# Plain-float32 scores beside their projections, step sizes transposed in two parts, and key ends packed over two heads

## The chip, the cores and the metric

The kernel runs as one launch on one core of a Trainium2 chip. The core has five engines that the profile names: PE (TensorE, the matrix engine; PEld is its loading of weights), DVE (VectorE), ACT (ScalarE), POOL (GpSimd) and SP (SyncE, which issues the DMAs here). The metric is the device time of one execution, in microseconds (us).

## The reference, cut to what matters

A block of two branches (compressed, selected and windowed attention, and a gated branch) is followed by two more layers: one with a state-space branch (called SSD below) and a 31-tap convolution, one with neighbourhood attention. Three places in it matter here.

```python
# first block: scores of every head against 15 compressed keys
s_cmp = einsum(q, k_cmp) * 64 ** -0.5          # 256 tokens, 16 heads in 2 key groups
# middle layer: step sizes of 2 directions x 32 heads, and their running sums
dt = softplus(h @ w_dt + dt_bias)              # 64 rows x 272 tokens
cs = cumsum(dt * -exp(A_log))                  # one direction runs backwards
# last layer, 32 heads of 64: a token sees the 16 columns around it, all 4 rows, and 16 meta tokens
s = q @ k.T * 64 ** -0.5 + bias                # -inf outside the neighbourhood
o = softmax(s) @ v
```

The batch is 1, the sequence 256 tokens on a grid of 4 rows and 64 columns, the meta tokens 16, the model width 2048; everything is float32.

## The kernel before, in words

Activations lie transposed, features on the 128 partitions and tokens along the free axis: 256 columns in the first block, 272 (16 meta tokens and 256) behind it. A **projection** is one block of 128 output features: `proj` (L135) runs 16 chunks of the contraction, and for each of them `mm3` (L118 to L122) issues three matmuls into one accumulator `acc`: high part by high part, low by high, high by low, all in float32r. The parts come from `load_piece` (L90): a DMA brings 8 chunks of raw weights, ACT copies them to `wh` (L98) and DVE subtracts to `wl` (L99). So a projection is 48 matmuls and two weight pieces, and one weight piece feeds 24 matmuls. Whatever else PE does stands between these matmuls in its list.

A tile scheduler turns the program text into one fixed instruction list for each engine. `K.run(gen, n)` lowers the priority of a small task by n instructions (`LATER`, 1000 and 1500), so that the scheduler lets it float in between later work. `tap` (L831) puts one of 480 VectorE taps of the 31-tap convolution behind each `wl`. PSUM has three `acc` tiles, two of tag "t", one of tag "o" and one of tag "s".

- **Scores of the compressed branch** (`block1`): keys stand in `kcbd`, block-diagonal over the two key groups, as a high and a low tile. Eight projections `pj(0.125)` make the queries; `K.split` parts each of them into `qh` and `ql`. Behind the last, 16 blocks (2 token tiles by 8 query blocks) of 3 matmuls each write 128 x 32 scores into `scps`: 48 matmuls.
- **Step sizes** (`layer_e`, generator `steps`): DVE works out `dt`, then `la`, two scans give `cs`; then both are transposed in one step into tiles `dtp`: each has two transposes (L803) and four small matmuls (L806) for the first 32 tokens. `dtT` and `dt0` are read by `decay` (L898) in the SSD stage, which runs from about 1200 to 1560 us.
- **`norm_out`** (L719): 16 multiplies on DVE (L721) and four stores, another task that floats.
- **Last layer** (`layer_o`): 16 head pairs, four projections each (q, k, v, z). Query tile 0 sees keys 0 to 175 and tile 1 keys 96 to 271 (`KR`): 176 keys a head, two heads block-diagonal, 352 columns of scores in `sp`, a softmax along the keys in `sb`. For the product with v the keys are cut in 128 and 48 (`VR`): four transposes of `vf` into `vt_ps`, eight of the probabilities into `pt_ps` (L1188, L1189), and eight matmuls (L1195), each of 64 output partitions (one head), into `o_ps`.

Of the kernel before, what the change touches and what calls it, by code (L numbers as in the profile page):

```python
# [19 lines left out]
P = 128  # L20
# [233 lines left out]
def block1(K, a):  # L254
# [4 lines left out]
    with ExitStack() as ctx:  # L259
# [123 lines left out]
        kcbd = [wk.tile([P, 2, 2, 16], F32R, tag="kcbd%d" % i, bufs=1, name="kcbd%d" % i) for i in range(2)]  # L383
        for i in range(2):
            nc.vector.memset(kcbd[i].bitcast(F32), 0.0)
# [19 lines left out]
        for g in range(2):  # L405
            gs = slice(64 * g, 64 * g + 64)
            K.split(kcbd[0][gs, :, g, 0:15], kcbd[1][gs, :, g, 0:15],
                    cps[gs, :32].rearrange("q (p n) -> q p n", p=2)[:, :, 0:15])
            for p in range(2):
                nc.vector.tensor_copy(hidbd[gs, p, :, g, 0:15], hs[gs, 1, p, None, 0:15].to_broadcast([64, 4, 15]))  # L410
# [25 lines left out]
        scps = K.ps.tile([P, 2, S], F32, tag="t", bufs=2, name="scps")  # L436
        for t in range(2):
            ts = slice(128 * t, 128 * t + 128)
            for j in range(8):
                p = j // 4  # L440
                K.mm3(scps[:, t, 32 * j : 32 * j + 32].rearrange("q (g n) -> q g n", g=2), qh[:, j, ts], ql[:, j, ts],
                      kcbd[0][:, p], kcbd[1][:, p], True, True)
# [235 lines left out]
def layer_e(K, a):  # L678
# [3 lines left out]
    with ExitStack() as ctx:  # L682
# [88 lines left out]

        def steps():
            nc.vector.tensor_scalar(s_, e, 2.0, None, op0=ALU.add)
            yield 1.0
            nc.vector.reciprocal(s_, s_)
            yield 1.0
            nc.vector.tensor_tensor(s_, s_, e, op=ALU.mult)
            yield 1.0
            nc.vector.tensor_tensor(s2, s_, s_, op=ALU.mult)
            yield 1.0  # L780
            nc.vector.tensor_scalar(pl, s2, 1.0 / 15, None, op0=ALU.mult)
            yield 1.0
# [12 lines left out]
            nc.vector.tensor_tensor_scan(cs[0:32, :], on[0:32, :], la[0:32, :], 0.0, op0=ALU.mult, op1=ALU.add)
            yield 1.0
            nc.vector.tensor_tensor_scan(cs[32:64, ::-1], on[32:64, :], la[32:64, ::-1], 0.0, op0=ALU.mult, op1=ALU.add)
            yield 1.0
            nc.sync.dma_start(csd, cs)
            for k, src in enumerate((dt, cs)):  # L800
                tp = K.ps.tile([P, 512], F32, tag="t", bufs=2, name="dtp")
                for i, (s0, s1) in enumerate(TT2[1:]):
                    nc.tensor.transpose(tp[:, 64 * i : 64 * i + 64], src[:, s0:s1], K.ident[:64, :64])  # L803
                for q in range(4):
                    r0 = 32 * (q // 2) + q % 2
                    nc.tensor.matmul(tp[32 * q : 32 * q + 32, 128:144], src[:, 0:32], K.ident[:64, r0 : r0 + 31 : 2],  # L806
                                     start=True, stop=True, skip_group_check=True)
                nc.scalar.activation(dtT[:, k].rearrange("p i r -> p (i r)"), tp[:, 0:128], AF.Copy)
                nc.scalar.activation(dt0[:, k], tp[:, 128:144], AF.Copy)
            yield 1.0  # L810
# [282 lines left out]
def layer_o(K, a, out):  # L1093
# [5 lines left out]
    KR = [(0, 176), (96, T2)]  # L1099
    VR = [(0, 128), (128, 176), (96, 224), (224, T2)]  # L1100
    with ExitStack() as ctx:
# [28 lines left out]

        for i in range(16):
            bias = wk.tile([P, 2, 2, 176], F32, tag="bias", name="bias")
# [16 lines left out]
            vf = k1("vf")  # L1149
            nc.vector.tensor_tensor(vf, vp, rb, op=ALU.mult)  # L1150
            vt_ps = K.ps.tile([P, 4, P], F32, tag="t", bufs=2, name="vt_ps")
            vt = wk.tile([P, 4, P], F32, tag="vt", name="vt")
            for j, (s0, s1) in enumerate(VR):
                nc.tensor.transpose(vt_ps[: s1 - s0, j, :], vf[:, s0:s1], K.ident)
            nc.scalar.activation(vt[:, 0::2, :], vt_ps[:, 0::2, :], AF.Copy)
            nc.scalar.activation(vt[:48, 1::2, :], vt_ps[:48, 1::2, :], AF.Copy)
# [9 lines left out]
            for t in range(2):  # L1166
                ts = slice(128 * t, 128 * t + 128)
                k0, k1_ = KR[t]
                K.mm3(sp[:, t, :352].rearrange("p (g k) -> p g k", g=2), qh[:, ts], ql[:, ts],
                      kb[:, 0, :, k0:k1_], kb[:, 1, :, k0:k1_], True, True)  # L1170
            sb = wk.tile([P, 2, 2, 176], F32, tag="sb", name="sb")
            nc.vector.tensor_tensor(sb.rearrange("p t g k -> p t (g k)"), sp[:, :, :352],
# [10 lines left out]
            for t in range(2):  # L1183
                ts = slice(128 * t, 128 * t + 128)
                pt_ps = K.ps.tile([P, 2, 2, P], F32, tag="t", bufs=2, name="pt_ps")
                for g in range(2):
                    nc.vector.tensor_scalar(sb[:, t, g], sb[:, t, g], rs[:, t, g : g + 1], None, op0=ALU.mult)
                    nc.tensor.transpose(pt_ps[:, 0, g, :], sb[:, t, g, 0:128], K.ident)  # L1188
                    nc.tensor.transpose(pt_ps[:48, 1, g, :], sb[:, t, g, 128:176], K.ident)  # L1189
                pt = wk.tile([P, 2, 2, P], F32, tag="pt", name="pt")  # L1190
                nc.scalar.activation(pt[:, 0], pt_ps[:, 0], AF.Copy)
                nc.scalar.activation(pt[:48, 1], pt_ps[:48, 1], AF.Copy)
                for kt, n in ((0, 128), (1, 48)):
                    for g in range(2):
                        nc.tensor.matmul(o_ps[64 * g : 64 * g + 64, ts], vt[:n, 2 * t + kt, 64 * g : 64 * g + 64], pt[:n, kt, g, :],  # L1195
                                         start=kt == 0, stop=kt == 1, skip_group_check=True)
# [52 lines left out]
def prep(inp):  # L1249
# [79 lines left out]
    o["rpb"] = np.ascontiguousarray(bias.reshape(16, 2, P, 2, 176).transpose(0, 2, 3, 1, 4))  # L1329
# [50 lines left out]
```

## Time and profile before

| | |
|---|---|
| median of 3 runs | 2284.5 us (2283.99 to 2286.28) |
| profiled execution | 2284.89 us, of which the span is 2283.1 us |
| granted TensorE clock, mean | 0.990 of full speed |
| busy share | PE 98%, PEld 95%, DVE 71%, ACT 51%, POOL 5% |
| DMA | 174 GB/s on average over the span |
| chain that ended last | 94% of it on PE, 3% DVE, 2% ACT |

A busy share is the time in which an engine had at least one instruction under way; PE's instructions overlap (a matmul of 256 columns is shown with 0.28 us, and the next starts 0.12 us behind it), so what a matmul costs is read from start to start. In the page's list of groups the time of one matmul is therefore longer than what it adds to the span. A plain-float32 matmul appears as two records where a float32r one appears as one.

### The profile page before, as it was taken

How to read it: one execution, taken by the hardware profiler on the slowest of the kernel's cores; microseconds unless marked ns; L12 is line 12 of the kernel's file. 1: busy time of each engine (PE TensorE's matmuls, PEld its weight loads, DVE VectorE, ACT ScalarE, POOL GpSimd, SP SyncE). 2: the span in 40 equal slices, each digit the busy share in tenths (PEclk: the TensorE clock that was granted, in tenths of full speed). 3: DMA queues.
4: the chain of work that ended last, by engine and by line, in shares of the span. 5: the costliest groups of instructions: out<-in, count | busy, mean ns of one | idle time of the engine just before them, and what ended most of it. 6: DMA issues, size and time to landing. Idle time of an engine off the chain costs nothing.

```text
span 2283.1 us, 44200 instructions
## 1 busy us (share of the span) xinstructions
PE 2229.3 (98%) x17798; PEld 2159.0 (95%) x17798; DVE 1628.3 (71%) x2840; ACT 1164.8 (51%) x2087; POOL 124.7 (5%) x119
## 2 busy tenths in 40 slices
PE   8999999999999999999998998899999999999997
PEld 6998799999999998999998998899999999999997
DVE  6567777555555669999999888798766555565554
ACT  4446644444444444445547887745444545454453
POOL 1000000000000130000000010002011000000011
PEclk9999999999999999999999999999999999999999
DMA  7642455555556555554554555354655555545453
GB/s 260 226 153 94 133 191 183 187 186 186 187 195 209 183 165 195 198 175 166 177 175 145 171 172 189 120 177 153 202 176 188 170 168 169 169 162 167 159 174 121
DMA packets 126413, 398.20 MB, mean 174 GB/s; under 512 B 16832, under 2 KB 33664, under 8 KB 125696
## 3 DMA queue, kind: packets, MB, share of 16 engines
q1 hardware_dynamic: 126064, 395.36, 52.5%
q8 instruction: 140, 2.29, 0.4%
q14 instruction: 65, 0.53, 0.1%
q10 hardware_dynamic: 144, 0.01, 0.0%
HBM read 390.92 MB, written 4.40 MB: 173 GB/s over the span
## 4 chain that ended last, share of the span: by engine, by line
PE 94%; DVE 3%; ACT 2%; issue 1%; DMA 0%; POOL 0%; SPq 0%; DVEq 0%; ACTq 0%; POOLq 0%
PE acc L120 29%; PE acc L122 28%; PE acc L121 28%; PE acc L156 2%; PE o_ps L1195 1%; PE yps L956 1%; DVE wl L99 1%; DVE vb L842 0%; PE pt_ps L503 0%; PE sp L120 0%; ACT wh L98 0%; PE sp L122 0%; PE sp L121 0%; PE o_ps L509 0%; DVE xin L291 0%
## 5 line engine op out<-in xcount | busy, mean ns | idle before, releaser
L98 ACT ACTIVATE wh<-raw 128x1024 fp32r<-128x1024 f32 x674 | 713.2, 1059 | 967.9 <-PE acc L121 575.6
L99 DVE TENSOR_TENSOR wl<-raw,wh 128x1024 fp32r<-128x1024 f32 x674 | 828.9, 1231 | 383.7 <-ACT wh L98 376.2
L120 PE MATMUL acc<-uh,wh 128*128 128x272 f32 (+1 forms) x1488 | 437.8, 294 | 15.7 <-DVE za L992 8.7
L122 PE MATMUL acc<-uh,wl 128*128 128x272 f32 (+1 forms) x1488 | 437.5, 294 | 0.0
L121 PE MATMUL acc<-ul,wh 128*128 128x272 f32 (+1 forms) x1488 | 435.1, 292 | 0.0
L121 PE MATMUL acc<-xl,wh 128*128 128x256 f32 (+1 forms) x1136 | 322.3, 284 | 0.0
L120 PE MATMUL acc<-xh,wh 128*128 128x256 f32 (+1 forms) x1136 | 322.2, 284 | 0.0
L122 PE MATMUL acc<-xh,wl 128*128 128x256 f32 (+1 forms) x1136 | 321.2, 283 | 0.0
L120 PEld LDWEIGHTS acc<-uh,wh 128*128 128x128 f32 (+1 forms) x1488 | 282.7, 190 | 21.5 <-DVE za L992 9.5
L121 PE MATMUL acc<-oul,wh 128*128 128x256 f32 (+1 forms) x1024 | 294.4, 287 | 0.0
L122 PE MATMUL acc<-ouh,wl 128*128 128x256 f32 (+1 forms) x1024 | 294.0, 287 | 0.0
L120 PE MATMUL acc<-ouh,wh 128*128 128x256 f32 (+1 forms) x1024 | 292.8, 286 | 0.0
L122 PEld LDWEIGHTS acc<-uh,wl 128*128 128x128 f32 (+1 forms) x1488 | 282.1, 190 | 3.5 <-issue 2.3
L121 PEld LDWEIGHTS acc<-ul,wh 128*128 128x128 f32 (+1 forms) x1488 | 282.4, 190 | 1.7 <-issue 0.8
L120 PEld LDWEIGHTS acc<-xh,wh 128*128 128x128 f32 (+1 forms) x1136 | 213.8, 188 | 1.2 <-DVE pj L316 0.4
L122 PEld LDWEIGHTS acc<-xh,wl 128*128 128x128 f32 (+1 forms) x1136 | 214.4, 189 | 0.2
L121 PEld LDWEIGHTS acc<-xl,wh 128*128 128x128 f32 (+1 forms) x1136 | 213.6, 188 | 0.7 <-issue 0.4
L122 PEld LDWEIGHTS acc<-ouh,wl 128*128 128x128 f32 x1024 | 192.6, 188 | 2.6 <-issue 2.6
L121 PEld LDWEIGHTS acc<-oul,wh 128*128 128x128 f32 x1024 | 192.7, 188 | 0.2
L120 PEld LDWEIGHTS acc<-ouh,wh 128*128 128x128 f32 x1024 | 192.8, 188 | 0.0
L842 DVE SCALAR_TENSOR_TENSOR vb<-early,par,vb 128x257 f32<-128x257 f32 (+9 forms) x330 | 148.4, 493 | 0.9 <-ACT vb L826 0.7
L204 POOL TENSOR_TENSOR sq<-sq 128x272 f32<-128x272 f32 (+1 forms) x44 | 48.5, 1103 | 747.5 <-ACT sq L201 746.7
(413 smaller groups left out, 4290.7 us busy)
## 6 DMA issues: line engine op xcount, KB each, us to landing
raw<-in_e_w_in SPq DMA_DIRECT2D x184, 512.0 KB, 4.0
raw<-in_w_in_fm SPq DMA_DIRECT2D x140, 512.0 KB, 3.9
raw<-in_o_w_in SPq DMA_DIRECT2D x128, 512.0 KB, 4.1
raw<-in_e_w_out SPq DMA_DIRECT2D x64, 512.0 KB, 4.5
raw<-in_w_up SPq DMA_DIRECT2D x32, 512.0 KB, 3.9
raw<-in_w_out SPq DMA_DIRECT2D x32, 512.0 KB, 4.4
raw<-in_w_pg SPq DMA_DIRECT2D x32, 512.0 KB, 3.8
raw<-in_o_w_out SPq DMA_DIRECT2D x32, 512.0 KB, 4.5
```

The lines of the kernel that those rows point to most:

```text
L98: nc.scalar.activation(wh, raw, AF.Copy)
L99: ins = nc.vector.tensor_tensor(wl, raw, wh.bitcast(F32), op=ALU.subtract)
L120: mm(out, lh, rh, start=start, stop=False)
L121: mm(out, lh, rl, start=False, stop=False)
L122: mm(out, ll, rh, start=False, stop=stop)
L156: self.nc.tensor.matmul(a, raws[c // 8][:, c % 8, :], x(c), start=c == 0, stop=c == 15)
L204: self.nc.gpsimd.tensor_tensor(acc, acc, sq, op=ALU.add)
L842: ins = nc.vector.scalar_tensor_tensor(v[:, lo:hi], u[:, lo + o : hi + o], par(K, "e_dw_w", 31 * b + k), v[:, lo:hi], op0=ALU.mult, op1=AL ...
L956: prev = nc.tensor.matmul(o, w, m, start=False, stop=k >= 6, skip_group_check=True).ins
L1195: nc.tensor.matmul(o_ps[64 * g : 64 * g + 64, ts], vt[:n, 2 * t + kt, 64 * g : 64 * g + 64], pt[:n, kt, g, :], start=kt == 0, stop=kt == 1 ...
```

## The change

Three edits. **Scores:** the compressed keys stay whole in one plain-float32 tile, and as soon as a query block `q` is there two plain-float32 matmuls (one for each token tile) make its scores; `qh` and `ql` are made as before, for the other branches.

```diff
-        kcbd = [wk.tile([P, 2, 2, 16], F32R, tag="kcbd%d" % i, bufs=1, name="kcbd%d" % i) for i in range(2)]
-        for i in range(2):
-            nc.vector.memset(kcbd[i].bitcast(F32), 0.0)
+        kcbd = wk.tile([P, 2, 2, 16], F32, tag="kcbd", bufs=1, name="kcbd")
+        nc.vector.memset(kcbd, 0.0)
...
-            K.split(kcbd[0][gs, :, g, 0:15], kcbd[1][gs, :, g, 0:15],
-                    cps[gs, :32].rearrange("q (p n) -> q p n", p=2)[:, :, 0:15])
+            nc.scalar.activation(kcbd[gs, :, g, 0:15], cps[gs, :32].rearrange("q (p n) -> q p n", p=2)[:, :, 0:15], AF.Copy)
...
         qh, ql = t8("h0", F32R, "qh"), t8("h1", F32R, "ql")
+
+        scps = K.ps.tile([P, 2, S], F32, tag="t", bufs=2, name="scps")
         for j in range(8):
-            K.split(qh[:, j, :], ql[:, j, :], pj(0.125))
+            q = pj(0.125)
+            K.split(qh[:, j, :], ql[:, j, :], q)
+            for t in range(2):
+                nc.tensor.matmul(scps[:, t, 32 * j : 32 * j + 32].rearrange("q (g n) -> q g n", g=2),
+                                 q[:, 128 * t : 128 * t + 128], kcbd[:, j // 4], start=True, stop=True)
 
 
         ptc = wk.tile([P, 2, S], F32, tag="ptc", bufs=1, name="ptc")
-        scps = K.ps.tile([P, 2, S], F32, tag="t", bufs=2, name="scps")
-        for t in range(2):
-            ts = slice(128 * t, 128 * t + 128)
-            for j in range(8):
-                p = j // 4
-                K.mm3(scps[:, t, 32 * j : 32 * j + 32].rearrange("q (g n) -> q g n", g=2), qh[:, j, ts], ql[:, j, ts],
-                      kcbd[0][:, p], kcbd[1][:, p], True, True)
```

**Step sizes:** `dt` is transposed as soon as it is there, `cs` behind the scans; the function does what the loop did.

```diff
+        def turned(k, src):
+
+            tp = K.ps.tile([P, 512], F32, tag="t", bufs=2, name="dtp")
+            for i, (s0, s1) in enumerate(TT2[1:]):
+                nc.tensor.transpose(tp[:, 64 * i : 64 * i + 64], src[:, s0:s1], K.ident[:64, :64])
+            for q in range(4):
+                r0 = 32 * (q // 2) + q % 2
+                nc.tensor.matmul(tp[32 * q : 32 * q + 32, 128:144], src[:, 0:32], K.ident[:64, r0 : r0 + 31 : 2],
+                                 start=True, stop=True, skip_group_check=True)
+            nc.scalar.activation(dtT[:, k].rearrange("p i r -> p (i r)"), tp[:, 0:128], AF.Copy)
+            nc.scalar.activation(dt0[:, k], tp[:, 128:144], AF.Copy)
+
...
+            turned(0, dt)
+            yield 1.0
             nc.scalar.activation(ea[:64], par(K, "A_log")[:64], AF.Exp)
             nc.vector.tensor_scalar(la, dt, ea[:64], -1.0, op0=ALU.mult, op1=ALU.mult)
...
-            for k, src in enumerate((dt, cs)):
-                tp = K.ps.tile([P, 512], F32, tag="t", bufs=2, name="dtp")
-                for i, (s0, s1) in enumerate(TT2[1:]):
...
-                nc.scalar.activation(dt0[:, k], tp[:, 128:144], AF.Copy)
+            turned(1, cs)
             yield 1.0
```

**Last layer:** each query tile sees 192 keys (0 to 191, 80 to 271) a head, the added ones masked by the bias. Each head has one block of 128 keys of its own; the 64 keys that are left of both heads are packed into one block of 128 by a value tile `vbd`, block-diagonal over the heads. So a tile needs three transposes of probabilities instead of four, and one output matmul of 128 partitions plus two of 64, instead of four of 64.

```diff
-    KR = [(0, 176), (96, T2)]
-    VR = [(0, 128), (128, 176), (96, 224), (224, T2)]
+    KR = [(0, 192), (80, T2)]
...
+        vbd = [big.tile([P, 2, P], F32, tag="vb%d" % i, name="vb%d" % i) for i in range(2)]
+        for i in range(2):
+            nc.gpsimd.memset(vbd[i], 0.0)
...
             vp = K.proj(a["o_w_in"][4 * i + 2], UH, UL, T2)
-            vf = k1("vf")
-            nc.vector.tensor_tensor(vf, vp, rb, op=ALU.mult)
+            vb = vbd[i % 2]
+            vf = k1("vf", 208)
+            for g in range(2):
+                gs = slice(64 * g, 64 * g + 64)
+                nc.vector.tensor_tensor(vf[gs], vp[gs, 64 * g : 64 * g + 208], rb[gs, 64 * g : 64 * g + 208], op=ALU.mult)
+                nc.vector.tensor_tensor(vb[gs, :, gs], two(vp[gs], 128 - 128 * g), two(rb[gs], 128 - 128 * g), op=ALU.mult)
             vt_ps = K.ps.tile([P, 4, P], F32, tag="t", bufs=2, name="vt_ps")
             vt = wk.tile([P, 4, P], F32, tag="vt", name="vt")
-            for j, (s0, s1) in enumerate(VR):
-                nc.tensor.transpose(vt_ps[: s1 - s0, j, :], vf[:, s0:s1], K.ident)
-            nc.scalar.activation(vt[:, 0::2, :], vt_ps[:, 0::2, :], AF.Copy)
-            nc.scalar.activation(vt[:48, 1::2, :], vt_ps[:48, 1::2, :], AF.Copy)
+            for t, (k0, k1_) in enumerate(KR):
+                nc.tensor.transpose(vt_ps[:, 2 * t, :], vf[:, 80 * t : 80 * t + P], K.ident)
+                nc.tensor.transpose(vt_ps[:, 2 * t + 1, :], vb[:, t, :], K.ident)
+            nc.scalar.activation(vt, vt_ps, AF.Copy)
...
                 k0, k1_ = KR[t]
-                K.mm3(sp[:, t, :352].rearrange("p (g k) -> p g k", g=2), qh[:, ts], ql[:, ts],
+                K.mm3(sp[:, t, :384].rearrange("p (g k) -> p g k", g=2), qh[:, ts], ql[:, ts],
                       kb[:, 0, :, k0:k1_], kb[:, 1, :, k0:k1_], True, True)
...
             for t in range(2):
                 ts = slice(128 * t, 128 * t + 128)
-                pt_ps = K.ps.tile([P, 2, 2, P], F32, tag="t", bufs=2, name="pt_ps")
+                pt_ps = K.ps.tile([P, 4, P], F32, tag="t", bufs=2, name="pt_ps")
                 for g in range(2):
                     nc.vector.tensor_scalar(sb[:, t, g], sb[:, t, g], rs[:, t, g : g + 1], None, op0=ALU.mult)
-                    nc.tensor.transpose(pt_ps[:, 0, g, :], sb[:, t, g, 0:128], K.ident)
-                    nc.tensor.transpose(pt_ps[:48, 1, g, :], sb[:, t, g, 128:176], K.ident)
-                pt = wk.tile([P, 2, 2, P], F32, tag="pt", name="pt")
-                nc.scalar.activation(pt[:, 0], pt_ps[:, 0], AF.Copy)
-                nc.scalar.activation(pt[:48, 1], pt_ps[:48, 1], AF.Copy)
-                for kt, n in ((0, 128), (1, 48)):
-                    for g in range(2):
-                        nc.tensor.matmul(o_ps[64 * g : 64 * g + 64, ts], vt[:n, 2 * t + kt, 64 * g : 64 * g + 64], pt[:n, kt, g, :],
-                                         start=kt == 0, stop=kt == 1, skip_group_check=True)
+                    nc.tensor.transpose(pt_ps[:, g, :], sb[:, t, g, 64 * g : 64 * g + P], K.ident)
+                nc.tensor.transpose(pt_ps[:, 2, :], sb[:, t].rearrange("p g k -> p (g k)")[:, 128:256], K.ident)
+                pt = wk.tile([P, 3, P], F32, tag="pt", name="pt")
+                nc.scalar.activation(pt, pt_ps[:, 0:3], AF.Copy)
+
+                nc.tensor.matmul(o_ps[:, ts], vt[:, 2 * t + 1, :], pt[:, 2, :], start=True, stop=False, skip_group_check=True)
+                for g in range(2):
+                    nc.tensor.matmul(o_ps[64 * g : 64 * g + 64, ts], vt[:, 2 * t, 64 * g : 64 * g + 64], pt[:, g, :],
+                                     start=False, stop=True, skip_group_check=True)
```

The bias is laid out for 192 keys instead of 176, and the sum with it, the maximum and the exponentials run over 192 keys.

The change moves instructions at three places. The first is PE in `block1`, at the end of a query projection. Before, the scores (`scps`) stand behind the end of the eighth:

```order
L122 MATMUL acc<-xh,wl 128x256
L120 MATMUL acc<-xh,wh 128x256
L121 MATMUL acc<-xl,wh 128x256
L122 MATMUL acc<-xh,wl 128x256
L120 MATMUL scps<-kcbd_609,qh 128x32
L121 MATMUL scps<-kcbd_610,qh 128x32
L122 MATMUL scps<-kcbd_609,ql 128x32
L120 MATMUL scps<-kcbd_609,qh 128x32
L121 MATMUL scps<-kcbd_610,qh 128x32
L122 MATMUL scps<-kcbd_609,ql 128x32
```

Now they stand in the row eight times, one pair of them 24 projection matmuls behind the end of the query projection that it reads (`pj` is the query block):

```order
L120 MATMUL acc<-xh,wh 128x256
L121 MATMUL acc<-xl,wh 128x256
L122 MATMUL acc<-xh,wl 128x256
L435 MATMUL scps<-kcbd,pj 128x32 x2
L120 MATMUL acc<-xh,wh 128x256
L121 MATMUL acc<-xl,wh 128x256
L122 MATMUL acc<-xh,wl 128x256
```

What moved: 48 float32r matmuls in three runs (21, 2 and 25, each 11 projection matmuls behind the one before) became eight places with two matmuls, 49 rows apart. The second place is PE in `layer_e`, where the step sizes are transposed (`dtp`). Before:

```order
L122 MATMUL acc<-uh,wl 128x272
L803 MATMUL dtp<-ident,early 128x64 x2
L806 MATMUL dtp<-ident,early 32x16 x3
L120 MATMUL acc<-uh,wh 128x272
L806 MATMUL dtp<-ident,early 32x16
L121 MATMUL acc<-ul,wh 128x272
L122 MATMUL acc<-uh,wl 128x272
L803 MATMUL dtp<-ident,early 128x64
L120 MATMUL acc<-uh,wh 128x272
L803 MATMUL dtp<-ident,early 128x64
L121 MATMUL acc<-ul,wh 128x272
```

And now, all twelve in one row, some 330 projection matmuls earlier in the program:

```order
L120 MATMUL acc<-uh,wh 128x272
L121 MATMUL acc<-ul,wh 128x272
L773 MATMUL dtp<-ident,early 128x64 x2
L776 MATMUL dtp<-ident,early 32x16 x4
L773 MATMUL dtp<-ident,early 128x64 x2
L776 MATMUL dtp<-ident,early 32x16 x4
L122 MATMUL acc<-uh,wl 128x272
L120 MATMUL acc<-uh,wh 128x272
```

What moved: the transposes stood in nine places with single projection matmuls between them and are now one run. The third place is DVE in `layer_e`, where `norm_out` (the lines with rbh) falls between two weight pieces (L99) and the taps. Before, it stands by the second GLU block, next to the first of the `steps` (the L773 of before):

```order
L842 SCALAR_TENSOR_TENSOR vb<-early,par,vb 128x257
L721 SCALAR_TENSOR_TENSOR x_8629<-x_8629,par,rbh 128x256 x4
L842 SCALAR_TENSOR_TENSOR vb<-early,par,vb 128x258
L721 SCALAR_TENSOR_TENSOR x_8629<-x_8629,par,rbh 128x256 x12
L842 SCALAR_TENSOR_TENSOR vb<-early,par,vb 128x259
L773 TENSOR_SCALAR early<-early 64x272
L842 SCALAR_TENSOR_TENSOR vb<-early,par,vb 128x260
L99 TENSOR_TENSOR wl<-raw,wh 128x1024
```

Now it stands 30 weight pieces later, among the taps:

```order
L844 SCALAR_TENSOR_TENSOR vb<-early,par,vb 128x268
L99 TENSOR_TENSOR wl<-raw,wh 128x1024
L844 SCALAR_TENSOR_TENSOR vb<-early,par,vb 128x268
L718 SCALAR_TENSOR_TENSOR x_8593<-x_8593,par,rbh 128x256 x5
L844 SCALAR_TENSOR_TENSOR vb<-early,par,vb 128x269
L718 SCALAR_TENSOR_TENSOR x_8593<-x_8593,par,rbh 128x256 x7
L844 SCALAR_TENSOR_TENSOR vb<-early,par,vb 128x269
L718 SCALAR_TENSOR_TENSOR x_8593<-x_8593,par,rbh 128x256 x4
L99 TENSOR_TENSOR wl<-raw,wh 128x1024
```

What moved: the same 16 multiplies now stand between two successive weight pieces, with three taps.

In the last layer the order round a head pair is as before but for the parts of the change: the three and three transposes of probabilities come in groups of one, three and two with one projection matmul (or two) between them, the four of the value tiles as one and three, and the six output matmuls in one row (one of 128 partitions, two of 64, and again).

## Rows read from the trace of the kernel before

**Rows 1.** The page, part 1: busy us (share) and instructions of an engine.
```profile
PE 2229.3 (98%) x17798; PEld 2159.0 (95%) x17798; DVE 1628.3 (71%) x2840; ACT 1164.8 (51%) x2087; POOL 124.7 (5%) x119
```

**Rows 2.** Stretches: length, busy us of PE, PEld, DVE, ACT, POOL, then PEclk, DMA.
```profile
100.00:140.00 40.00, 40.00 (x340) 40.00 (x340) 23.13 (x30) 17.29 (x22) 0.00 (x0) 1.00 0.56 188
900.00:1200.00 300.00, 300.00 (x2378) 298.43 (x2378) 285.77 (x507) 141.99 (x199) 6.94 (x9) 0.99 0.55 182
1040.00:1100.00 60.00, 60.00 (x482) 60.00 (x481) 56.20 (x98) 28.52 (x35) 1.62 (x2) 1.00 0.54 180
1200.00:1560.00 360.00, 332.96 (x2553) 315.62 (x2552) 311.10 (x626) 253.89 (x587) 35.86 (x36) 0.97 0.50 158
1760.00:2190.00 430.00, 430.00 (x3560) 416.07 (x3559) 251.62 (x391) 213.95 (x426) 0.00 (x0) 1.00 0.51 166
```

**Rows 3.** Stretches, same columns: the one that holds the compressed scores.
```profile
143.84:157.46 13.62, 13.62 (x95) 13.62 (x94) 5.20 (x8) 2.42 (x3) 0.00 (x0) 0.75 0.25 87
```

**Rows 4.** Timeline of PE, two small plain-float32 matmuls: start us, us, what.
```profile
86.24 0.28 PE L120 MATMUL acc<-xh,wh 128*128 128x256 f32 x1
86.36 0.55 PE L413 MATMUL vcps<-w,hidbd 128*128 128x64 f32 x4
86.72 0.37 PE L121 MATMUL acc<-xl,wh 128*128 128x256 f32 x1
86.92 0.28 PE L122 MATMUL acc<-xh,wl 128*128 128x256 f32 x1
```

**Rows 5.** Stretches: the one that holds the transposes of the step sizes.
```profile
1027.11:1035.06 7.95, 7.95 (x48) 6.46 (x47) 7.95 (x19) 4.96 (x15) 0.00 (x0) 0.79 0.27 92
```

**Rows 6.** Timeline of PE, start of those transposes.
```profile
1027.23 0.29 PE L122 MATMUL acc<-uh,wl 128*128 128x272 f32 x1
1027.45 0.33 PE L803 MATMUL dtp<-ident,early 64*128 64x64 f32 x2
1027.71 0.24 PE L806 MATMUL dtp<-ident,early 64*32 64x16 f32 x6
1027.89 0.39 PE L120 MATMUL acc<-uh,wh 128*128 128x272 f32 x1
1028.21 0.23 PE L806 MATMUL dtp<-ident,early 64*32 64x16 f32 x2
```

**Rows 7.** Timeline of PE, last layer: around eight transposes of the probabilities.
```profile
1964.99 0.29 PE L120 MATMUL acc<-ouh,wh 128*128 128x272 f32 x1
...
1966.12 0.29 PE L122 MATMUL acc<-ouh,wl 128*128 128x272 f32 x1
```

**Rows 8.** Timeline of PE, last layer: around the output matmuls of one head pair.
```profile
1968.62 0.29 PE L121 MATMUL acc<-oul,wh 128*128 128x272 f32 x1
1968.83 1.54 PE L1195 MATMUL o_ps<-pt,vt 128*64 128x128 f32 x16
...
1970.54 0.29 PE L120 MATMUL acc<-ouh,wh 128*128 128x272 f32 x1
```

**Rows 9.** Timeline of PE, first block: transposes between two groups of half-width matmuls.
```profile
219.26 0.44 PE L503 MATMUL pt_ps<-ident,sb 128*128 128x128 f32 x2
219.63 0.66 PE L509 MATMUL o_ps<-pt,vsw 128*64 128x128 f32 x8
```

**Rows 10.** Timeline of PE, last layer: first score matmul, projection behind the six.
```profile
1982.68 0.33 PE L120 MATMUL sp<-kb,qh 128*128 128x352 f32 x1
...
1983.66 0.28 PE L120 MATMUL acc<-ouh,wh 128*128 128x256 f32 x1
```

**Rows 11.** Timeline of VectorE, last layer: the value block scaled.
```profile
1976.75 0.44 DVE L1150 TENSOR_TENSOR vf<-acc,rb 128x272 f32<-128x272 f32 x1 [0.77 <-PE acc L122]
```

**Rows 12.** Timeline of PE, last layer: its four transposes.
```profile
1979.53 0.60 PE L1154 MATMUL vt_ps<-ident,vf 128*128 128x128 f32 x4
```

**Rows 13.** Line 721 on VectorE: duration ns min/median/max, first and last start us.
```profile
L721 DVE SCALAR_TENSOR_TENSOR x<-x,par,rbh x16: 475/476/477, 880.8 to 887.2; 128x256 f32<-128x256 f32 x16
```

**Rows 14.** Waits of PE: for whom, us in total, times, longest us.
```profile
PE yps L956 <- DVE m L904: 5.8, 2, 4.1
```

More of the change, by code (lines that the diff above doesn't have):

```diff
@@ L799, in steps @@
             nc.sync.dma_start(csd, cs)
-            for k, src in enumerate((dt, cs)):
-                tp = K.ps.tile([P, 512], F32, tag="t", bufs=2, name="dtp")
-                for i, (s0, s1) in enumerate(TT2[1:]):
[L803 to L808, printed above, removed]
-                nc.scalar.activation(dt0[:, k], tp[:, 128:144], AF.Copy)
+            turned(1, cs)
             yield 1.0
@@ L1129, in layer_o, with two @@
             nc.gpsimd.memset(kbd[i].bitcast(F32), 0.0)
+        vbd = [big.tile([P, 2, P], F32, tag="vb%d" % i, name="vb%d" % i) for i in range(2)]
+        for i in range(2):
+            nc.gpsimd.memset(vbd[i], 0.0)
+        def two(v, o):
+            v = v[:, o : o + 64]
+            return bass.AP(tensor=v.tensor, offset=v.offset, ap=[v.ap[0], [80, 2], [1, 64]])
         for i in range(16):
-            bias = wk.tile([P, 2, 2, 176], F32, tag="bias", name="bias")
+            bias = wk.tile([P, 2, 2, 192], F32, tag="bias", name="bias")
             nc.sync.dma_start(bias, a["rpb"][i])
@@ L1168, in layer_o @@
                 k0, k1_ = KR[t]
[L1169 removed]
+                K.mm3(sp[:, t, :384].rearrange("p (g k) -> p g k", g=2), qh[:, ts], ql[:, ts],
                       kb[:, 0, :, k0:k1_], kb[:, 1, :, k0:k1_], True, True)
[L1171 to L1172 removed]
+            sb = wk.tile([P, 2, 2, 192], F32, tag="sb", name="sb")
+            nc.vector.tensor_tensor(sb.rearrange("p t g k -> p t (g k)"), sp[:, :, :384],
                                     bias.rearrange("p t g k -> p t (g k)"), op=ALU.add)
@@ L1320, in prep @@
     rpb = g["o_rpb_2"][0]
-    bias = np.zeros((32, P, 2, 176), f32)
-    for t, (q0, k0) in enumerate(((0, 0), (144, 96))):
+    bias = np.zeros((32, P, 2, 192), f32)
+    for t, (q0, k0) in enumerate(((0, 0), (144, 80))):
         qr, qc = row[q0 : q0 + 128, None], col[q0 : q0 + 128, None]
-        kr, kc = row[None, k0 : k0 + 176], col[None, k0 : k0 + 176]
+        kr, kc = row[None, k0 : k0 + 192], col[None, k0 : k0 + 192]
         st = np.clip(qc - 8, 0, 48)
@@ L1328, in prep @@
         bias[:, :, t] = np.where(kc < 0, f32(0), np.where(ok, b, f32(-1e30)))
-    o["rpb"] = np.ascontiguousarray(bias.reshape(16, 2, P, 2, 176).transpose(0, 2, 3, 1, 4))
+    o["rpb"] = np.ascontiguousarray(bias.reshape(16, 2, P, 2, 192).transpose(0, 2, 3, 1, 4))
     o["c_ident"] = np.eye(P, dtype=f32)
```

## The prediction

> **What bounds the kernel now.** The page's busy shares come first: PE is busy 98% of the span [rows 1], and the chain that ended last is PE for 94%. A share over the whole span hides the stages, so the second view is the table of stretches [rows 2]. In the last layer (1760 to 2190) PE is busy 430.00 of 430 us at a granted clock of 1.00, and DVE only 251.62; there, PE time taken away comes off the span one for one, until another engine is late. From 900 to 1200 PE is busy without a gap and DVE 285.77 of 300: DVE has 14.2 us to spare. From 1200 to 1560, the SSD stage, PE stands still 360 - 332.96 = 27 us and the clock is 0.97: 3% below the upper level of 2.4 GHz is 6% of the time, 22 us, at the lower of 1.2 GHz, which costs about 11 us. That stage has real waits, the longest of one kind 4.1 us for the DVE product `m` [rows 14].
>
> The price of PE work is read from start to start: a projection matmul of 256 columns takes 40/340 = 0.1176 us, one of 272 columns 60/482 = 0.1245 us [rows 2]. What a block costs is its stretch less the projection matmuls in it. Two stretches stand out, since PE is busy throughout and the granted clock is yet low: 0.75 where the scores lie [rows 3], 0.79 where the step sizes are transposed [rows 5].
>
> **Scores.** The stretch is 13.62 us with 95 records, 48 of them scores; 47 projections take 5.53, so the scores cost 8.1 us [rows 3]. A mean of 0.75 says that half the stretch, 6.8 us, ran at 1.2 GHz: 3.4 us lost; the scores alone would be 4.7. The change puts in eight places of two plain-float32 matmuls. The nearest rows are two such matmuls of 64 columns, four records: from 86.24 to 86.92, less two projections, 0.445 us [rows 4]; eight times that is 3.6. Each place is too short to be a stretch of its own kind, with 48 projections between, so I take no clock loss. **-4.5 us.** Bounds: if the 3.4 us are lost all the same, -1.1; at the old 4.7/48 = 0.098 for each of 32 records, 3.1, thus -5.0. The wait it adds is PE's for the query block `q`: DVE scales it while 24 projection matmuls run (2.8 us), and DVE is idle 42% in the stretch nearby, 16.87 of 40 us [rows 2]. Were it late, the projection behind it would wait too. The `scps` tile now holds one of two "t" tiles for 40 us, but no other "t" tile is asked for between its first and last block. The smaller work on ACT and DVE for the keys lies beside PE.
>
> The Trainium skill ("FP8 and Floating Point Precision", TensorE Precision Notes) speaks against the edit: true FP32 takes four passes. The trace shows two records, not four, for a plain-float32 matmul [rows 4]; by the page this would be 64 passes in place of 48.
>
> **Step sizes.** The stretch is 7.95 us with 48 records, 20 of them transposes and small matmuls; 28 x 0.1245 = 3.49, so they cost 4.46, of which the clock of 0.79 (42% of the stretch at 1.2 GHz, 3.3 us) makes 1.7 [rows 5]. Now it is one run of 20 records. In its opening a transpose takes 0.13 ((1027.71 - 1027.45)/2) and a small record 0.03 ((1027.89 - 1027.71)/6) [rows 6]; 4 x 0.13 + 16 x 0.03 = 1.0, and going in, between the two tiles and out again I estimate 0.5, since 8 records with two projections between 1027.23 and 1028.21 cost 0.73: 1.5 in all. **-3.0 us.** Bounds: -1.3 if the clock falls all the same; -3.5 without the 0.5. The run stands some 330 projections (41 us) earlier in PE's row, near 985 us; what it reads comes from the scans, which stand over twenty weight pieces (60 us) before it in DVE's row, so PE doesn't wait. The four ACT copies behind it have 200 us until `decay`.
>
> **Last layer, per head pair.** Eight transposes of probabilities take (1966.12 - 1964.99) - 0.25 = 0.88, 0.11 each [rows 7]; two go: -0.22. The value tiles keep four transposes [rows 12]. Eight output matmuls, 16 records, take (1970.54 - 1968.62) - 0.25 = 1.67 [rows 8]. Now it is full, two half, full, two half. A full one costs 0.22 beside the stream, half of the 0.445 above [rows 4]; two full ones ahead of a half-width group take 219.63 - 219.26 = 0.37 [rows 9], so a change of width costs 0.15 beside 0.22. Half-width pairs at the old 1.67/4 = 0.42 and full ones at 0.22 and 0.37 give 1.43; with leaving, 1.5. -0.17, bounds 0 (the change of width eats it) and -0.35. Score matmuls widen from 352 to 384 columns: six take 1983.66 - 1982.68 = 0.98, 0.163 each [rows 10]; 96 columns over a projection cost 0.046, so 32 cost 0.015, six +0.09. Sum -0.30, by 16: **-4.8 us**, bounds -2.1 and -7.7.
>
> What is hidden: the value block becomes four DVE operations instead of one of 0.44 [rows 11], at an estimate 1.3 us (each on 64 partitions, but priced by its columns: 208, 208, 128, 128). It ended at 1977.19 and its first transpose started at 1979.53 [rows 11, 12]: 2.3 us of cover, of which 0.9 goes. Without cover it would be 0.9 x 16 = 14 us. Softmax over 192 keys is 9% more on an engine idle 41% there [rows 2]. ACT has fewer copies, POOL is idle, and bias grows by 9% on DMA queues busy 51%.
>
> **What moves along.** `norm_out` is 16 x 0.476 = 7.6 us of DVE [rows 13]. It now stands between two weight pieces with three taps: about 10.3 us with the piece itself, against four prefetched pieces of 24 x 0.1245 = 3.0 us each, 12 us. That is enough, with 1.7 to spare; if fewer than four are ready, PE waits up to 2 us. Its four stores on SP's queue move with it, each behind its four products; weight loads behind them wait for no more than that. I take 0.
>
> **Sum.** -4.5 - 3.0 - 4.8 = -12.3 on the profiled execution of 2284.9 (span 2283.1 and 1.8 around it): 2272.6. The median lies 0.4 lower than that execution: **2272.2 us**, and by the bounds above 2268 to 2280; its own likely range is 2268 to 2276.
>
> **Rivals.**
> - The clock falls anyway. In both stretches PE was busy whole, and yet at the lower level; what sets it isn't shown, so the loss may come with the other work near them. -12.3 + 3.4 + 1.7 = -7.2: 2277.3. For it: nothing in either stretch names the cause. Against it: like stretches of projections alone are at 1.00 [rows 2]. Chance 0.10. The Trainium skill ("TensorE: Matmul & The Clock Gate", What's actually happening) ties the lower clock to PE being idle; these rows do not agree, with PE busy 13.62 of 13.62 us; by the page the block would not have cost the clock, and this rival's time follows.
> - More waits in the SSD stage. Order on DVE, ACT and PE is nearly as before there, but shifted a little against the weight pieces. A wait of 4.1 us [rows 14] with its share of the clock loss (11/27) is 5.8. One more: 2278.0 (0.08); two more: 2283.8 (0.08); one or two fewer: 2266.4 or 2260.6 (0.12 together).
> - Slower. DVE enters the SSD stage late: the lump of `norm_out` now comes 75 us nearer to it, DVE had 14.2 us to spare from 900 to 1200 [rows 2], and from the point where those are used up every `m` and `wl` comes late, and PE waits at `yps` pair after pair. Three waits more are 17.4: 2289.6. Against it: the total of DVE's work there is as before. Chance 0.05.
> - The plain-float32 scores don't save. Four passes of 0.111 for each of 16 matmuls are 7.1 instead of 3.6: 2275.7. The records speak against it. Chance 0.02.
>
> **How the numbers follow.** The forecast has 0.55. The measurement can tell 0.2% from no change, 4.6 us: faster is below 2279.9, slower above 2289.1. Faster: 0.55 + 0.10 + 0.08 + 0.12 + 0.02 = 0.87; same: 0.08; slower: 0.05. The range 2262 to 2282 leaves out the two cases above it (0.13) and the better half of the fewer waits.
>
> **What would show it.** Right: granted clock 1.00 from 140 to 160 us, eight places of four `scps` records that add 0.45 each; one run of `dtp` near 985 us that adds 1.5, clock 1.00; in the last layer a head pair shorter by 0.30 us, an output group of 1.5 and score matmuls 0.178 apart, PE busy without a gap. Wrong: a gap of PE before `vt_ps` or behind `norm_out`, an output group of 1.67 or more, a clock below 0.9 in either place, or an idle sum of PE from 1200 to 1560 that differs from 27 us by 4 or more.

## The result and the profile after

The changed kernel takes 2271.23 us (median of 4 runs, 2269.26 to 2272.87) against 2284.24: ratio 0.9942, 95% interval 0.9925 to 0.9959. The forecast was 2272.2. In a second set of five runs, e4 below, the ratio is 0.9938 (0.9925 to 0.9951).

The profiled execution took 2269.26 us, span 2267.5. The page's line of engines, which answers to [rows 1]:

```profile
PE 2217.6 (98%) x17686; PEld 2151.1 (95%) x17686; DVE 1641.9 (72%) x2885; ACT 1161.4 (51%) x2037; POOL 131.5 (6%) x121
```

PE is still busy 98%: 11.7 us of its work are gone and 3.9 us of its standing still. The stretches that answer to [rows 2, 3, 5] are: the eight query projections with their scores; the one with the transposes and norm_out; the SSD stage from the first `cbps` to the first `lnv`; the last layer.

```profile
98.00:152.00 54.00, 54.00 (x460) 54.00 (x460) 29.75 (x39) 22.26 (x28) 0.00 (x0) 1.00 0.52 174
960.00:1000.00 40.00, 40.00 (x333) 39.66 (x332) 37.43 (x69) 21.94 (x40) 0.00 (x0) 1.00 0.67 238
1189.65:1562.28 372.63, 349.01 (x2692) 331.21 (x2691) 321.65 (x642) 259.23 (x594) 40.04 (x37) 0.98 0.51 165
1748.00:2176.00 428.00, 428.00 (x3478) 418.64 (x3477) 265.48 (x438) 212.04 (x379) 0.00 (x0) 1.00 0.49 167
```

Look first at the granted clock, the third number from the end of a line: 1.00 in the first two, where it was 0.75 and 0.79 [rows 3, 5], and PE busy without a gap beside norm_out (16 products from 972.1 to 978.8 us). The SSD stage before, between the same two instructions, had 27.04 us of idle PE; now 372.63 - 349.01 = 23.62:

```profile
1196.97:1574.71 377.74, 350.70 (x2692) 333.29 (x2691) 321.24 (x644) 261.17 (x596) 37.87 (x37) 0.97 0.51 163
```

Three places on PE's timeline, for the terms of the sum. First a place with scores, which stands for eight:

```profile
107.17 0.28 PE L122 MATMUL acc<-xh,wl 128*128 128x256 f32 x1
107.29 0.53 PE L435 MATMUL scps<-kcbd,pj 128*128 128x32 f32 x4
107.65 0.36 PE L120 MATMUL acc<-xh,wh 128*128 128x256 f32 x1
```

The transposes of the step sizes:

```profile
981.69 0.29 PE L121 MATMUL acc<-ul,wh 128*128 128x272 f32 x1
981.91 0.33 PE L773 MATMUL dtp<-ident,early 64*128 64x64 f32 x2
982.17 0.25 PE L776 MATMUL dtp<-ident,early 64*32 64x16 f32 x8
982.36 0.33 PE L773 MATMUL dtp<-ident,early 64*128 64x64 f32 x2
982.62 0.25 PE L776 MATMUL dtp<-ident,early 64*32 64x16 f32 x8
982.80 0.40 PE L122 MATMUL acc<-uh,wl 128*128 128x272 f32 x1
```

And the output matmuls of one head pair (answering to [rows 8]):

```profile
1792.04 0.29 PE L121 MATMUL acc<-oul,wh 128*128 128x272 f32 x1
1792.16 0.38 PE L1207 MATMUL o_ps<-pt,vt 128*128 128x128 f32 x2
1792.47 0.44 PE L1209 MATMUL o_ps<-pt,vt 128*64 128x128 f32 x4
1792.85 0.49 PE L1207 MATMUL o_ps<-pt,vt 128*128 128x128 f32 x2
1793.26 0.44 PE L1209 MATMUL o_ps<-pt,vt 128*64 128x128 f32 x4
1793.63 0.39 PE L122 MATMUL acc<-ouh,wl 128*128 128x272 f32 x1
1793.86 0.29 PE L120 MATMUL acc<-ouh,wh 128*128 128x272 f32 x1
```

To compare stages in kernels whose order differs, I used the names of six tiles as marks. I took the starts of the first `hps`, `ptps`, `cbps`, `lnv`, `oss` and `fss` on PE, counted the projection matmuls between them in PE's row, and took off 0.1176, 0.1245 or 0.230 us for each (256, 272 or 512 columns). What is left of each stage, in us, one profiled execution each (the tail runs from `fss` to the end; differences in the text are taken before rounding):

| kernel | to `hps` | scores, to `ptps` | step sizes, to `cbps` | SSD, to `lnv` | last layer, `oss` to `fss` | tail |
|---|---|---|---|---|---|---|
| before | 28.0 | 15.9 | 90.8 | 93.0 | 67.6 | 9.9 |
| after | 28.4 | 11.2 | 87.7 | 87.9 | 63.9 | 10.4 |
| e4, after again | 27.6 | 11.2 | 87.7 | 87.9 | 63.9 | 10.4 |
| e1, scores | 27.6 | 11.2 | 87.8 | 91.0 | 67.6 | 10.4 |
| e2, step sizes | 30.7 | 15.9 | 90.3 | 96.5 | 67.6 | 9.9 |
| e3, last layer | 29.2 | 15.9 | 90.7 | 93.0 | 63.9 | 10.4 |
| e5, float32r by block | 29.4 | 13.2 | 88.3 | 94.6 | 67.6 | 9.9 |
| e6, plain late | 28.2 | 11.1 | 87.2 | 93.8 | 67.6 | 9.9 |
| e7, all full | 27.6 | 11.2 | 87.8 | 88.0 | 60.3 | 10.1 |
| e12, e7 again | 29.2 | 11.2 | 86.0 | 90.7 | 60.3 | 10.4 |
| e8, norm_out early | 27.7 | 11.2 | 91.9 | 92.0 | 63.9 | 10.4 |
| e9, one run | 29.7 | 15.9 | 87.1 | 96.4 | 67.6 | 9.9 |

e2's row is from a long execution, 2290.69 us. Scores and last layer repeat to 0.1 us. The SSD stage does not: from 87.9 to 96.5, and the same kernel (e7, e12) has 88.0 and 90.7. The first column differs by execution too, and ahead of every edit: from 20 to 30 us the granted clock was 0.83 in e2, e3, e5, e9 and e12, whose values there are 29.2 or more, and 1.00 in the others.

### The profile page after: what moved, and what is told of

The parts are those of the page before. It is cut to its first block, busy times and chain, and to the rows that moved or that the text cites. A ratio compares the mean times of both kernels' runs of the same rounds, so it can differ in the third digit from the quotient of the medians.

```text
span 2267.5 us, 43976 instructions
## 1 busy us (share of the span) xinstructions
PE 2217.6 (98%) x17686; PEld 2151.1 (95%) x17686; DVE 1641.9 (72%) x2885; ACT 1161.4 (51%) x2037; POOL 131.5 (6%) x121
## 4 chain that ended last, share of the span: by engine, by line
PE 94%; DVE 3%; ACT 1%; DMA 1%; issue 0%; SPq 0%; POOL 0%; DVEq 0%; ACTq 0%; POOLq 0%
PE acc L120 29%; PE acc L122 29%; PE acc L121 28%; PE acc L156 2%; PE yps L958 1%; DVE wl L99 1%; PE o_ps L506 1%; PE pt_ps L500 1%; PE o_ps L1209 1%; PE sp L120 0%; PE sp L122 0%; PE sp L121 0%; PE o_ps L1207 0%; DVE xin L291 0%; DVE vb L844 0%
## 5 line engine op out<-in xcount | busy, mean ns | idle before, releaser
L99 DVE TENSOR_TENSOR wl<-raw,wh 128x1024 fp32r<-128x1024 f32 x674 | 829.9, 1232 | 400.0 <-ACT wh L98 395.3
L120 PE MATMUL acc<-uh,wh 128*128 128x272 f32 (+1 forms) x1488 | 436.6, 293 | 14.2 <-DVE za L994 11.1
```

Of the source, the lines that this page charges most:

```text
L99: ins = nc.vector.tensor_tensor(wl, raw, wh.bitcast(F32), op=ALU.subtract)
L120: mm(out, lh, rh, start=start, stop=False)
```

## Experiments

Times are medians against the kernel before, measured beside them: 2283.97 us for e1 to e4, 2283.83 for e5 to e8, 2283.03 for e9. e10, e11 and e12 have one run each.

**The three edits, one at a time, and all of them again.** e1 is the first edit shown above alone, e2 the second, e3 the third (with the bias laid out for it), e4 the changed kernel.

> Only the scores edit, on the kernel before. Theory A (the cost lies where the order of PE puts the work): this edit alone also gathers the transposes of the step sizes into one run and moves norm_out by 30 weight pieces, as in the changed kernel, since the scheduler's offsets count instructions; so it holds the term of the scores (-4.1 to -4.5 us), that of the step sizes (-3.0 to -3.5) and whatever the SSD stage gains (0 to -4): 8 to 11 us faster, ratio 0.9952 to 0.9965. Theory B (each edit earns its own term): -4.5 us, ratio 0.9980, and the transposes still cost 4.5 us at a low clock.

> Only the step sizes transposed in two parts. Theory A: PE's order keeps them in nine places among single projection matmuls, so nothing changes: within 1 us of before, granted clock near 0.8 there as before. Theory B (the edit itself gathers them): 3 us faster, ratio 0.9987.

> Only the last layer's packed key ends. Theory A: -0.26 us for each of 16 head pairs, as the changed kernel's trace has it, -4.1 us, ratio 0.9982, and nothing else moves. Rival: part of the 13 us comes from here by way of fewer instructions on ACT, then -6 or more, ratio 0.9974 or lower.

> The changed kernel once more beside the three parts. If the parts add, its gain is the sum of e1, e2 and e3; by the prediction -12.3 us, ratio 0.9946 (range 0.994 to 0.995). If the SSD stage's 4 us in the one profile were chance, the median gain is near 11.5 us and this profile's SSD stage has PE idle 26 to 27 us again; if they belong to the kernel, idle 23 to 24 us.

e1: 2275.14 us, 8.8 less, ratio 0.9959 (0.9948 to 0.9971). e2: 2281.83, 0.9994 (0.9984 to 1.0005). e3: 2280.29, 0.9983 (0.9974 to 0.9991). e4: 2268.51, 0.9938. The three gains add to 0.41 + 0.06 + 0.17 = 0.64%, e4 has 0.62%. Theory A holds for the places: the scores edit alone carries its own term and that of the step sizes (15.9 to 11.2 and 90.8 to 87.8), and the step-size edit alone leaves the transposes in seven pieces (eight before, by the trace, not nine), as its timeline shows (the first lines with `dtp`). Its total decides nothing, since the 0.9987 of theory B lies in its interval; its trace does, with a granted clock of 0.79 from 1029.79 to 1038 us:

```profile
1030.01 0.33 PE L776 MATMUL dtp<-ident,early 64*128 64x64 f32 x2
1030.27 0.25 PE L779 MATMUL dtp<-ident,early 64*32 64x16 f32 x8
...
1031.02 0.27 PE L776 MATMUL dtp<-ident,early 64*128 64x64 f32 x1
...
1031.55 0.27 PE L776 MATMUL dtp<-ident,early 64*128 64x64 f32 x1
...
1032.08 0.23 PE L779 MATMUL dtp<-ident,early 64*32 64x16 f32 x2
...
```

The reason that I gave for it in e1, that the scheduler counts instructions, falls with e5: that kernel has as many score instructions as before, in another order, and its transposes are gathered too. e4's SSD stage has 372.60 - 349.03 = 23.6 us of idle PE again.

**What takes the clock down at the scores.** e5 keeps float32r and spreads the matmuls:

```diff
         for j in range(8):
             K.split(qh[:, j, :], ql[:, j, :], pj(0.125))
+            for t in range(2):
+                ts = slice(128 * t, 128 * t + 128)
+                p = j // 4
+                K.mm3(scps[:, t, 32 * j : 32 * j + 32]..., qh[:, j, ts], ql[:, j, ts], kcbd[0][:, p], kcbd[1][:, p], True, True)
```

> The kernel before with its 48 float32r score matmuls kept, but issued block by block behind each query projection (16 places of three); PE's order gathers the step sizes' transposes and moves norm_out as in the changed kernel. Theory A (the clock falls where many matmuls of 32 columns stand close together, whatever their type): no low clock there, 16 places of 0.34 us = 5.4 instead of 8.1, so 1.8 us more than the plain-float32 form's 3.6; in all 6 to 9 us faster than before, ratio 0.9961 to 0.9974. Theory B (float32r with its three terms costs the clock): the granted clock falls again around the query projections and the scores cost 8 us or more.

e6 takes the plain-float32 form and puts it behind the eighth projection; e10 and e11 issue each of its matmuls twice and four times (shown against e1, and shortened):

```diff
             K.split(qh[:, j, :], ql[:, j, :], q)
-            for t in range(2):
-                nc.tensor.matmul(...)
+            nc.gpsimd.tensor_copy(qw[:, j, :], q)
+        for t in range(2):
+            for j in range(8):
+                for rep in range(n):       # n = 1 (e6), 2 (e10), 4 (e11)
+                    nc.tensor.matmul(..., qw[:, j, 128 * t : 128 * t + 128], kcbd[:, j // 4], start=True, stop=True)
```

> The scores edit with its 16 plain-float32 matmuls issued behind the eighth projection, in runs of 7 and 9 (a copy of the queries on GpSimd keeps them until then). 32 records of 0.1 us are 3.2 to 3.6 us at the full clock. Theory A: so many matmuls of 32 columns together take the clock down at least once, 1.7 us or more lost, 5 to 7 us in all. Theory B (the plain form alone is what helps): 3.6 us, clock 1.00, and the time of e1.

> As e6, with each of the 16 plain-float32 score matmuls issued twice (the same values into the same place): runs of 28 and 36 records a few projections apart. Theory A (it is the amount of such work in one place): the granted clock falls to half there, 7.1 us at the full clock become 9 or more. Theory B (plain float32 doesn't cost the clock): clock 1.00 and 7.1 us.

> As e6, with each score matmul issued four times: 128 records in one run. Theory A: the clock falls, 14.2 us at the full clock become 18 or more. Theory B: clock 1.00, 14.2 us.

The stretches of the four, in that order, each with its scores (the stretch, its length, PE's busy time; the third number from the end is the granted clock):

```profile
100.00:160.00 60.00, 60.00 (x512) 60.00 (x511) 33.53 (x46) 23.59 (x31) 0.00 (x0) 1.00 0.50 168
```

```profile
143.60:152.00 8.40, 8.40 (x75) 8.40 (x74) 3.74 (x6) 2.42 (x3) 0.40 (x1) 1.00 0.39 129
```

```profile
145.00:162.00 17.00, 17.00 (x98) 17.00 (x97) 5.88 (x12) 3.05 (x4) 0.40 (x1) 0.61 0.19 65
```

```profile
145.00:170.00 25.00, 25.00 (x134) 25.00 (x133) 2.08 (x4) 1.36 (x2) 0.40 (x1) 0.57 0.13 48
```

e5's scores keep the full clock: 16 places, of two and four matmuls in turn, that cost 8 x 0.22 + 8 x 0.45 = 5.4 us, as theory A said. e6's too, and there theory A was wrong: 14 and 18 records close together are not enough, 3.6 us. With 64 and 128 records the clock falls although the type is the same, and PE is busy all the time: e11's one run,

```profile
145.25 0.28 PE L122 MATMUL acc<-xh,wl 128*128 128x256 f32 x1
145.37 24.50 PE L439 MATMUL scps<-kcbd,qw 128*128 128x32 f32 x128
169.68 0.56 PE L120 MATMUL acc<-xh,wh 128*128 128x256 f32 x1
```

takes 24.3 us where 14.2 was the price at the full clock. So the type alone does not decide; the clock fell in the stretches with 48 (float32r) [rows 3], 64 and 128 such records, and not in that with 32. For the clock, each half of the scores edit is enough: spreading the work (e5), or the plain form with its fewer records (e6). Whether in e6 it is the number or the type isn't shown: no run has 32 float32r records in one place, or 48 plain ones. e10 and e11 took 2288.72 and 2299.68 us. e6: 2277.36, 0.9961 (0.9949 to 0.9974).

e5's total misses its range: 2281.92 us, 0.9991 (0.9982 to 1.0), though the stages of the scores and the step sizes are 5.2 us shorter than before. In its one profile the SSD stage is 1.6 us longer and the start 1.4; the start is the clock of that execution (0.83 from 20 to 30 us, above).

**Whether norm_out's place or the gathered transposes set the SSD stage's time.** e8 is the changed kernel with `LATER = [0, 1500]`; e9 is the kernel before with the transposes raised in priority:

```diff
-            for k, src in enumerate((dt, cs)):
+            with tc.high_priority(offset=3000):
+                for k, src in enumerate((dt, cs)):
```

> The changed kernel with LATER[0] = 0: norm_out stands at its old place by the second GLU block, and the step sizes' transposes are again split over seven places, 336 projections later. Theory: of the 13 us the scores (4.5) and the last layer (4.1) stay; the transposes cost 3.4 us more at a low clock, and the SSD stage, whose waits follow DVE's order, loses the 2 to 5 us that it gained, PE idle from the first cbps to yss 22 to 23 us instead of 19.5: ratio 0.9958 to 0.9972. Rival (the SSD stage's waits don't hang on norm_out): only the transposes come back, idle stays at 19.5, ratio 0.9953 to 0.9957.

> The kernel before, with only the step sizes' transposes raised in priority, so that they stand as two runs of ten records in PE's row (26 projection matmuls apart) and norm_out stays in its place. Theory (the pieces between single projections cost the time, and the lower clock with them): 1.3 us instead of 4.5, granted clock 1.00 there, 3.0 to 3.4 us faster than before, ratio 0.9985 to 0.9987. Rival (the gain in that stage came with norm_out's move): no change, 0.9996 to 1.0004.

e8: 2276.86 us, 0.9968 (0.9955 to 0.998), inside the theory's range; its interval still touches the rival's (0.9953 to 0.9957). Idle PE up to `yss` is 20.9 us, neither 19.5 nor 22 to 23, so neither account has it right. And the price of 4.2 us ahead of the stage is another than I said: PE waits 2.1 us more there, and the pieces cost 2 us more at a clock that does not fall. e9's transposes are two runs of 0.65 us:

```profile
912.70 0.33 PE L804 MATMUL dtp<-ident,early 64*128 64x64 f32 x2
912.97 0.25 PE L807 MATMUL dtp<-ident,early 64*32 64x16 f32 x8
...
916.61 0.33 PE L804 MATMUL dtp<-ident,early 64*128 64x64 f32 x2
916.87 0.25 PE L807 MATMUL dtp<-ident,early 64*32 64x16 f32 x8
```

Its stage is 3.6 us shorter, as expected, and the kernel is no faster: 2284.91 us, 1.0007 (0.9998 to 1.0016). The time comes back in the SSD stage:

```profile
1195.18:1576.40 381.22, 351.99 (x2692) 334.56 (x2691) 321.26 (x646) 261.52 (x596) 37.86 (x37) 0.97 0.51 161
```

381.22 - 351.99 = 29.2 us idle against 27.0, and PE's own work takes 352.0 against 350.7. Its waits, and behind them those after the change (answering to [rows 14]), in us in total, times, longest:

```profile
PE acc L120 <- DVE za L993: 9.3, 2, 6.9
PE acc L120 <- DVE cacc L874: 7.3, 4, 2.4
PE yps L957 <- DVE m L905: 4.8, 3, 2.7
PE acc L120 <- ACT zb L1041: 3.1, 1, 3.1
```

```profile
PE acc L120 <- DVE za L994: 11.1, 3, 5.3
PE yps L958 <- DVE m L906: 4.7, 2, 2.9
PE acc L120 <- DVE cacc L875: 3.1, 3, 1.8
```

It is not a debt that DVE brings into the stage: the 366th `wl` ends 6.0 us ahead of the first `cbps` before and after the change and in e1, 5.9 in e9.

Nor do the two things of this heading decide it together. e5 and e6 have both, the transposes in one run (985 and 981 us) and norm_out beside it (975 and 971), and idle PE of 27.0 and 25.8 us in the stage. What the traces do show is a fourth place that the change moves, beside the three shown ahead of the prediction: the order inside the SSD stage. Of its 402 PE instructions that are not projection matmuls, 192 stand 11 to 48 projection matmuls from their old place. e1, e4, e7 and e12 have exactly the order of the changed kernel, and idle PE of 23.6 us (24.9 in e12); e3 has exactly that of the kernel before, and 27.0 like it; e2, e5, e6, e8 and e9 have each one of their own, and 25.0 to 29.2. The clock goes with the execution: in that one order the stage's granted clock is 0.98 in three executions and 0.97 in e1 and e12, and PE's work in it takes 349.0 us after the change and 352.1 in e1. Which of the moves frees the waits is open.

**A version beyond both.** In the changed kernel's group above, a full matmul ahead of a half-width pair takes 0.31 or 0.41 us. e7 is the changed kernel with all output matmuls over 128 partitions; each head's own block meets a value tile whose other half is zero:

```diff
-                nc.tensor.matmul(o_ps[:, ts], vt[:, 2 * t + 1, :], pt[:, 2, :], start=True, stop=False, ...)
-                for g in range(2):
-                    nc.tensor.matmul(o_ps[64 * g : 64 * g + 64, ts], vt[:, 2 * t, 64 * g : 64 * g + 64], pt[:, g, :], ...)
+                for g in range(3):
+                    nc.tensor.matmul(o_ps[:, ts], vt[:, t, g, :], pt[:, g, :], start=g == 0, stop=g == 2)
```

> The changed kernel with all six output matmuls of a head pair over 128 output partitions (each head's own 128 keys against a value tile whose other 64 columns are zero; one more ACT copy and a third more value tile). Theory: the half-width matmuls cost 0.37 to 0.41 a pair of them with the change of width, a full one 0.22; six full ones 1.33 to 1.4 us against 1.57, 16 times 0.2 = 3 to 4 us faster than the changed kernel, ratio to before 0.992 to 0.9925. Rival (the two widths run beside each other, so only the count of records matters, 12 in both): the time of the changed kernel, 0.9938 to 0.9942.

```profile
1764.23 0.29 PE L121 MATMUL acc<-oul,wh 128*128 128x272 f32 x1
1764.36 1.50 PE L1214 MATMUL o_ps<-pt,vz 128*128 128x128 f32 x12
1765.62 0.37 PE L122 MATMUL acc<-ouh,wl 128*128 128x272 f32 x1
1765.82 0.29 PE L120 MATMUL acc<-ouh,wh 128*128 128x272 f32 x1
```

1765.82 - 1764.23 less two projections is 1.34 us against 1.57. e7 takes 2264.75 us, 0.9917 (0.9903 to 0.993): 3.8 us below e4, 16 x 0.23, the fastest here. e12 is one more execution of the same kernel:

> The kernel of e7 once more, with a profile, beside the others: if the SSD stage's idle PE time belongs to the kernel and not to the execution, 19.5 us between the first cbps and yss again, and the last layer the same to 0.1 us; if it is chance, 21 us or more.

2267.59 us. Last layer 60.3 again; idle PE from `cbps` to `yss` 20.8 instead of 19.5, between the two expectations, so the SSD stage's time belongs to the execution as well as to the kernel.

## Why the prediction was right or wrong

The total came out within 1 us of the first median and 3.7 above the second, and the mechanism, PE time taken away, was right. That it came so close is in part luck: the three terms made -11.4 instead of -12.3 us in the profile, and the SSD stage gave 5.1 us that the forecast did not have. Step by step:

- **Scores**: 0.45 us a place (107.65 - 107.17 less one projection is 0.36, and the projection behind takes 0.09 more), 3.6 in all, clock 1.00; -4.7 by the table, -4.5 forecast. No wait for `q`.
- **Step sizes**: 982.80 - 981.69 less one projection is 0.99, with the next projection 1.10, where I took 1.5, so the place alone gave 3.4; the stage round it gave -3.0 by the table, -3.0 forecast. I had put this to the step-size edit. It belongs to the scores edit, whose order gathers the transposes; the edit "in two parts" alone is worth nothing that shows (e2).
- **Last layer**: -3.7 by the table and by e3, -4.8 forecast. The mis-sized term is the output group: 1.57 instead of 1.5, since a full matmul between half-width pairs took 0.41, where I had 0.37, and the first of them, ahead of a change too, 0.31 where I had 0.22; the half-width pairs, 0.38 and 0.37 where I had 0.42, gave part of it back. Transposes 0.11 each in groups as in one run, score matmuls 0.176 apart ((1806.52 - 1805.64)/5), 0.178 forecast. The cover of the value block held: its four products took from 1772.56 to 1773.73, 1.17 us, and PE is busy 428.00 of 428.
- **"I take 0" for what moves along**: right for norm_out, at which PE doesn't wait (its products overlap, and the 16, with two taps among them, took 7.2 us, where I had added up their durations to 7.6 without taps). Wrong for the SSD stage, where I took the order as nearly the same, only shifted a little, and gave fewer waits a chance of 0.12: half of its small PE instructions moved, and it is 5.1 us shorter in two executions (idle 27.0 to 23.6, the rest clock). With +0.5 in the tail this makes -15.6 of the profiled execution; the median of the first set is 13.0 less. Where its longer executions (up to 2272.87) lost their time isn't shown, since only one was profiled; in e7 and e12, one kernel, the start and the SSD stage differ by 1.6 and 2.7. Idle PE changed by 3.4, short of the 4 that I had set as a sign of being wrong, though the stage had changed.
- **The sentence that fails** is "PE time taken away comes off the span one for one", used beyond the last layer. Ahead of the SSD stage a saving may be kept (e1, e4) or taken back (by the medians, e9 all of its 3.6 us, e5 some 3 of its 5.2). The scheduler makes an order of its own for that stage in e1, e5 and e9, and the 23.6 us of idle PE come with one such order. Why that order waits less is open; DVE's lead at the entry, norm_out's place and the gathered transposes don't give it.
- **Rivals**: the clock did not fall anyway, and the scores cost no 7.1 us. But the argument from "two records, not four" was not sound: it counted records, and where the operand is wide a plain record takes nearly twice as long as a float32r one, so a matmul 3.6 times as long (last section). "Fewer waits" came beside the forecast, not in its place.

## What to carry to other kernels

Whether small matmuls should stand together is read from the trace, not from a rule: 48 float32r scores cost 8.1 us together, with the clock low, and 5.4 spread (e5), while the twenty records of the transposes cost 4.5 us in pieces and 1.1 in one run. An edit in one place may gather or scatter work in another by the scheduler, so read the new order before a gain is put to an edit. In a stage that waits, a few us saved ahead of it are worth nothing certain: judge the edit by its own stage, and the total by several runs. Two half-width matmuls side by side took 0.37 or 0.38 us, a full one among its kind 0.22, so half the output width saves little; where zeros can fill it up, the full one saves the change of width (1.34 us instead of 1.57 a head pair).

## What the runs showed of the hardware

- PE busy 25.00 of 25 us at a granted clock of 0.57, with 128 records of 32 columns in a row and no wait: half the clock's rate without idleness. The stretch of e6, with 32 such records, stays at 1.00, those with 48 float32r ones [rows 3] and 64 plain ones (e10, 0.61) do not. The Trainium skill ("TensorE: Matmul & The Clock Gate", What's actually happening) ties the clock to how busy PE has been; by the profile's busy share, which is whole here, the trace does not agree.
- A plain-float32 matmul with fresh 128 x 128 weights is two records of 0.11 us each, whether its other operand has 32, 64 or 128 columns (0.45 for four records of 32 and of 64 columns, 1.34 for twelve of 128), so here four records replace six float32r ones of the same 0.11. That holds for narrow operands only. With 272 columns a plain record takes 0.226 us ((890.95 - 876.49)/64, the clock at 1.00), so a matmul of two records 0.45, against 0.1245 for a float32r one:

```profile
876.49 14.83 PE L156 MATMUL acc<-uf,rawf 128*128 128x272 f32 x64
890.95 0.49 PE L120 MATMUL acc<-uh,wh 128*128 128x272 f32 x1
```

- A change of output width cost 0.1 to 0.2 us here: a full matmul with a half-width pair behind it takes 0.31 or 0.41 from start to start, one in a row of its kind 0.22 (1.34/6).
